# Two parts of a layer's modulation move into another stage, and their working room with them

## The chip, the core and the metric

The kernel runs on one core of a Trainium2 chip. Its engines work side by side, each through its own queue in order: TensorE (PE) does the matmuls, VectorE (DVE) and ScalarE (ACT) do element-wise work, GpSimd (POOL) takes some of it from VectorE, and SyncE (SP) issues nearly all transfers. The metric is the device time of one execution in microseconds, and lower is better.

## The reference, cut to what matters

One transformer block (gated delta net and dilated attention, then a feed-forward part) is followed by two layers on a stream of 512 tokens and a context of 256 tokens, both 1024 wide. Each of the two layers is modulated by six vectors, which come from a condition vector c for the stream and another for the context:

```python
for layer in range(DEPTH_2):
    mod_l = (jax.nn.silu(c) @ w_ada[layer] + b_ada[layer])[:, None, :]
    mod_c = jax.nn.silu(c_ctx) @ w_ada[layer] + b_ada[layer]
    sh1_l, sc1_l, g1_l, sh2_l, sc2_l, g2_l = jnp.split(mod_l, 6, axis=-1)
    ...
    h_l = modulate(x_l, sh1_l, sc1_l)     # rms_norm(x) * (1 + scale) + shift
    h_c = modulate(x_c, sh1_c, sc1_c)
    ...                                   # mixer: layer 0 even, layer 1 odd
    x_l = x_l + g1_l * y_l
    x_l = x_l + g2_l * conv_ffn(modulate(x_l, sh2_l, sc2_l), ...)
```

The product with w_ada is a matrix (6144 x 1024) times two vectors. All values are float32.

## The kernel before

**Layout and matmuls.** Streams lie feature-major: 1024 features are eight tiles of 128 partitions, with tokens along the free side. A float32 product is made of three matmuls of split values (high by high, high by low, low by high), lines L323, L324 and L325 in `mm3`. `wchunk` fetches 128x1024 weights (512 KB) into `wraw` (two buffers) and splits them into `whi` (ACT, L311) and `wlo` (POOL, L312; three buffers each). A chunk serves 24 matmuls of 512 columns.

**Stages in order.** `block1_mixer` makes the first block's projections and its two attentions. Behind the delta net's projections stand `dilated_bias` (a table that goes through DRAM into `dstrip`, 2 MB), `hyena_mlp` (three rounds of a small matmul, a sine whose argument is reduced by seven DVE steps, and ACT's sine `fh`; its weights are `fw`) and `dilated_proj` (`dq`, `dk` by DVE, `dv` by ACT). `block1_tail` makes the context's normalised and modulated input `hc`, the hyena filter's taps (`hyena_taps`), the output projection (`out_proj`), the norm behind it (`post_norm`, with two spectra of the taps on PE), and the first feed-forward part: four groups of 6, 6, 5 and 5 hidden tiles, each with its gate and up products (24 matmuls each) and then eight down products. In this part `x` is the residual stream, 16 KB a partition, that the part's own norm adds to at its end. `even_mixer` follows: six projections token-major (`qk_gemm` and `qk_post` for queries and keys, with squares on ACT L1361 and their sums on DVE L1363), then the attentions. Then come `out_and_ffn` for layer 0, the odd mixer, and `out_and_ffn` for layer 1.

**The modulation.** `ada(pool, parts)` is a generator. It loads c for both streams to all partitions (1 MB), makes the silu (four steps on ACT L1081 and DVE L1082), and for each part (a third of a layer: 16 tiles of 128 outputs) fetches 32 pieces of w_ada of 256 KB and reduces each with both vectors on DVE (L1090: `ada_j` and `ada_w` are the two outputs, which nobody reads; the sum goes to `ada_p`). A part has 64 reductions in 16 steps of four. Three buffers of `ada_w` turn round, so a load on SP waits for a reduction.

**Beside.** `with self.beside(steps, rate, skip)` makes each `wchunk` that ticks add `rate` to a count, and each whole unit takes a step of the generator. `issue_after` keeps the step's instructions behind the latest instruction of their engine at that point. What is left at the end of the `with` is emitted there. The tile framework orders instructions by a simulated timeline, so the order on an engine isn't only that of the program. Before, part (0,0) runs beside `dilated_proj` at 4 steps a tick, parts (0,1) and (0,2) beside the even mixer's projections at 3 a tick, and layer 1's three parts beside layer 0's `out_and_ffn` at 0.8 a tick.

Of the kernel before, what the change touches and what calls it, by code (L numbers as in the profile page):

```python
# [2 lines left out]

# [219 lines left out]
class Prog:  # L223
# [225 lines left out]
    def block1_mixer(self, hp, psd):  # L449
        V, S, G, PE, Q, A = self.V, self.S, self.G, self.PE, self.Q, self.A  # L450
        h = hp.tile([P, 2, KD, T], F32R, name="h", tag="hx")
        with self.pools(p1=1) as (pp,):
            rb = pp.tile([P, T], F32, name="rb")
            with self.pools(g0=1) as (gp,):
                es = ExitStack()
                self.banks = {"mm": 4, "g": 4, "p": 3, "c": 1, "o": 1, "a": 2, "pv": 1}
                with self.pools(psA=1) as (ps,):
                    act = self.acts(h, 0, T)
                    da = self.pool(es, "da")
                    with self.pools(ad=1, gp1=1) as (ad, gt), ExitStack() as xs:  # L460
                        xp = self.pool(xs, "x0", side="right")
                        x = xp.tile([P, KD, T], F32, name="x")
                        acc = xp.tile([P, T], F32, name="acc")
                        Q.dma_start(self.sm, A["small"])
                        first = [self.wchunk(A["w1_qkv"][0], eng=V)]
                        for k in range(KD):
                            (Q if k % 2 else S).dma_start(x[:, k], A["xT"][k * P:(k + 1) * P])
                        first.append(self.wchunk(A["w1_qkv"][1]))
                        for k in range(KD):
                            g = self.vec("g_mix_pre", k)  # L470
                            S.activation(h[:, 0, k], x[:, k], AF.Copy, scale=g)
                            V.scalar_tensor_tensor(out=h[:, 1, k], in0=x[:, k], scalar=g,
                                                   in1=h.bitcast(F32)[:, 0, k], op0=ALU.mult, op1=ALU.subtract)

                        def stats():
                            self.load_consts()
                            for k in range(KD):
                                accs = self.sqacc(xp, acc, x[:, k], k, eng=V, bufs=2)
                            r = self.token_rstd(pp, ps, accs, 4, "g")
                            pb = self.bank(ps, "g")  # L480
                            self.bcast_all(pb, r, 4)
                            S.activation(rb, pb, AF.Copy)
                            return r

                        r = self.gdn(gp, gt, ps, rb, stats, act, self.tiles_of(h), first)
                        self.dilated_bias(ps)
                        with self.beside(self.ada(ad, [(0, 0)]), 4, 0, self.mark):
                            self.tick()
                            with self.pools(hm=1) as (hm,):
                                self.hyena_mlp(hm, ps)  # L490
                            self.dilated_proj(da, ps, rb, r, act, self.tiles_of(h))
                om = hp.tile([P, 2, KD, T], F32R, name="h", tag="hx")
                with self.pools(psA2=1, gt=1) as (ps, gt):
                    with self.pools(db2=1) as (db,), ExitStack() as pd:
# [25 lines left out]
    def gdn(self, gp, gt, ps, rb, stats, act, tiles, first):  # L520
# [49 lines left out]
        for mi in range(12):  # L570
# [2 lines left out]
            conv(mi)  # L573
            if mi == 1:
                self.gdn_gates(gp, gt, ps, rb, act)
            if mi == 11:
                self.mark = self.latest(V)
            if mi:
                turn(mi - 1)
        sg = self.sg = gp.tile([P, 4, T], F32, name="sgate")  # L580
# [391 lines left out]
    def block1_tail(self, hp, ps, om, begun, x, hc):  # L972

        V, S, G, PE, Q, A = self.V, self.S, self.G, self.PE, self.Q, self.A
        with self.pools(t1=1, tt=2) as (tp, tt):
            es = ExitStack()
            hf = self.pool(es, "hf")
            y = tp.tile([P, KD, T], F32, name="y")
            xc = y[:, 0:4].rearrange("p a (b t) -> p (a b) t", b=2)
            Q.dma_start(xc, A["cT"].rearrange("(k p) t -> p k t", p=P))  # L980
            accc = hf.tile([P, C], F32, name="accc")
            for k in range(KD):
                accs = self.sqacc(tt, accc, xc[:, k], k)
            self.modulate(tt, ps, xc, accs, hc, 0, 0, 1)
            self.hyena_taps(tp, hf, ps)
            acc = tp.tile([P, T], F32, name="acc")
            act = self.acts(om, 0, T)
# [23 lines left out]
            es.close()  # L1011
            tf = self.pool(es, "tf", 2)
            act = self.acts(h, 0, T)
            m0 = 0
            for ng in FFN_GROUPS:
                fa = []
                for m in range(m0, m0 + ng):
# [14 lines left out]
                    self.split(a[:, 0], a[:, 1], g)  # L1032
                    fa.append((a[:, 0], a[:, 1]))
                last = m0 + ng == MF
                for m in range(KD):
                    w = self.wchunk(A["w1_d"][m][:, m0 * P:(m0 + ng) * P], ng * P)
                    p = self.bank(ps, "mm")
# [10 lines left out]
            self.dump("x1", x)  # L1048
            es.close()
            return r  # L1050

    def post_norm(self, tt, ps, accs, acc, y, x, rp, spec, then=None):

# [14 lines left out]
        return r  # L1068


    def ada(self, pool, parts):

        V, S, Q, A = self.V, self.S, self.Q, self.A
        c = pool.tile([P, 2, D], F32, name="ada_c")
        junk = pool.tile([P, T], F32, name="ada_j")
        raw = lambda: pool.tile([P, T], F32, name="ada_w", bufs=3)
        Q.dma_start(c.rearrange("p s k -> p (s k)"), A["c_row"].to_broadcast([P, 2 * D]))
        for s in range(2):
            for i in range(2):
# [46 lines left out]
    def modulate(self, tt, ps, x, accs, h, layer, i0, s, r=None, st="t"):  # L1126
# [1 line left out]

        V, S = self.V, self.S
        mod = self.mods[layer]  # L1130
        n = x.shape[2]
        if r is None:
            r = self.token_rstd(tt, ps, accs, n // P, st)
        rb = self.bank(ps, st)
# [1 line left out]
        for k in range(KD):  # L1136
            tmp = tt.tile([P, T], F32, name="md")
            sh = mod[:, i0 * 8 + k, s:s + 1]
            V.scalar_tensor_tensor(out=tmp[:, :n], in0=x[:, k], scalar=mod[:, (i0 + 1) * 8 + k, s:s + 1],
                                   in1=rb[:, :n], op0=ALU.mult, op1=ALU.mult)  # L1140
            S.activation(h[:, 0, k], tmp[:, :n], AF.Identity, bias=sh)
            V.scalar_tensor_tensor(out=h[:, 1, k], in0=tmp[:, :n], scalar=sh, in1=h.bitcast(F32)[:, 0, k],  # L1142
# [279 lines left out]
    def even_mixer(self, hp, ps, psd, hs, first):  # L1422
# [5 lines left out]
        with self.pools(em=1) as (em,):  # L1428
# [12 lines left out]
            with self.pools(ei=1, et=2) as (ei, tt):  # L1441
# [12 lines left out]
                for g, dst, gain, tab in ((0, qa, gq, None), (1, ka, gk, None), (3, qkb, dq, tq), (4, qkb, dk, tk),  # L1454
# [25 lines left out]

                        post = None
                    jobs.append((gemm, post))
                with self.pools(ad2=1) as (ad,), self.beside(self.ada(ad, [(0, 1), (0, 2)]), 3):
                    self.pipeline(jobs)
            psd.close()
            oms = [self.new_h(hp, s) for s in range(2)]
# [593 lines left out]
```

## Time and profile before

| | us |
|---|---|
| median of 3 runs | 2619.76 (2618.95 to 2622.86) |
| the profiled execution | 2619.97 |
| its span in the profile | 2618.2 |
| PE busy | 2474.6 (95%) |
| DVE busy | 1631.3 (62%) |
| ACT busy | 993.6 (38%) |
| POOL busy | 1194.1 (46%) |
| reductions of the modulation on DVE | 189.7 + 179.9 |

The span is what the trace covers. The busy shares are means over stages that differ, so stages are read one by one. A wait names the engine or transfer that came last.

### The profile page before, as it was taken

To read this page: it belongs to the slowest core of one execution; us is meant where nothing else is said; L and a number is where in the kernel's file an instruction comes from. 1 tells how busy PE (TensorE), PEld (TensorE's weight loads), DVE (VectorE), ACT (ScalarE), POOL (GpSimd) and SP (SyncE) were. 2 spreads that over 40 slices of the span, in tenths; PEclk is the share of its full clock that TensorE was granted. 3 is DMA by queue.
4 is the path that set the end of the run, shared out by engine and by line. 5 is a ranking of instruction groups with operands and counts; after the bars stand their busy time and mean duration, and the time that the engine had idled before them with its cause. 6 is when DMAs were issued, how large, how long until landed. Compare 5 with 4: busy or idle time off the path is not lost.

```text
span 2618.2 us, 35313 instructions
## 1 busy us (share of the span) xinstructions
PE 2474.6 (95%) x13312; PEld 2051.2 (78%) x13312; DVE 1631.3 (62%) x2896; ACT 993.6 (38%) x1763; POOL 1194.1 (46%) x835
## 2 busy tenths in 40 slices
PE   7888999899999988987999999999999999999999
PEld 5766876788888766766788888888888888788887
DVE  6987656645334698868747677868667456534333
ACT  4434534422224422367734212122234563323232
POOL 3346535555556444577724233333245427344443
PEclk9988999899999998998999999999999999999999
DMA  5252022222322333400132333434232114232322
GB/s 197 73 187 67 26 63 97 81 93 92 104 94 91 141 129 126 164 15 26 51 113 97 107 132 117 132 108 140 87 115 84 49 42 142 84 97 87 103 94 96
DMA packets 103453, 257.94 MB, mean 99 GB/s; under 512 B 11745, under 2 KB 20065, under 8 KB 102900
## 3 DMA queue, kind: packets, MB, share of 16 engines
q1 hardware_dynamic: 102708, 254.64, 29.0%
q8 instruction: 105, 1.72, 0.3%
q10 hardware_dynamic: 576, 1.05, 0.1%
q14 instruction: 64, 0.52, 0.1%
HBM read 246.06 MB, written 14.83 MB: 100 GB/s over the span
## 4 chain that ended last, share of the span: by engine, by line
PE 72%; DVE 16%; DMA 3%; ACT 3%; issue 3%; POOL 3%; SPq 0%; POOLq 0%; DVEq 0%; ACTq 0%
PE ps_mm L323 14%; PE ps_mm L325 14%; PE ps_mm L324 14%; PE ps_mx L324 3%; PE ps_mx L325 3%; PE ps_mx L323 3%; PE ps_m L324 3%; PE ps_m L323 3%; PE ps_m L325 3%; PE ps_pv L1596 2%; DVE ada_j L1090 2%; PE ps_s L1589 2%; DVE ada_w L1090 2%; PE ps_t L435 2%; DMA ada_w<-in_w_ada 2%
## 5 line engine op out<-in xcount | busy, mean ns | idle before, releaser
L312 POOL TENSOR_TENSOR wlo<-wraw,whi 128x1024 fp32r<-128x1024 f32 (+2 forms) x344 | 778.0, 2265 | 1102.7 <-ACT whi L311 1026.8
L311 ACT ACTIVATE whi<-wraw 128x1024 fp32r<-128x1024 f32 (+2 forms) x345 | 336.9, 978 | 949.0 <-PE ps_mm L324 480.9
L323 PE MATMUL ps_mm<-h,whi 128*128 128x512 f32 (+1 forms) x1496 | 541.3, 363 | 11.8 <-ACT whi L311 7.2
L325 PE MATMUL ps_mm<-h,wlo 128*128 128x512 f32 (+1 forms) x1496 | 540.4, 362 | 2.0 <-POOL wlo L312 2.0
L324 PE MATMUL ps_mm<-h,whi 128*128 128x512 f32 (+1 forms) x1496 | 540.5, 362 | 1.1 <-DVE h L1142 1.0
L323 PEld LDWEIGHTS ps_mm<-h,whi 128*128 128x128 f32 x1496 | 282.8, 189 | 56.9 <-ACT whi L311 7.2
L325 PEld LDWEIGHTS ps_mm<-h,wlo 128*128 128x128 f32 x1496 | 282.4, 189 | 48.9 <-POOL wlo L312 2.6
L324 PEld LDWEIGHTS ps_mm<-h,whi 128*128 128x128 f32 x1496 | 282.5, 189 | 47.6 <-issue 1.7
L1090 DVE CUSTOM_DVE_ANT_0 ada_j<-ada_w,ada_c 128x512 f32<-128x512 f32 x192 | 189.7, 988 | 13.7 <-DMA ada_w<-in_w_ada 13.3
L324 PE MATMUL ps_mm<-fa,whi 128*128 128x512 f32 (+1 forms) x528 | 187.6, 356 | 0.0
L325 PE MATMUL ps_mm<-fa,wlo 128*128 128x512 f32 (+1 forms) x528 | 186.3, 356 | 1.0 <-POOL wlo L312 1.0
L323 PE MATMUL ps_mm<-fa,whi 128*128 128x512 f32 (+1 forms) x528 | 185.8, 356 | 0.0
L1090 DVE CUSTOM_DVE_ANT_0 ada_w<-ada_w,ada_c 128x512 f32<-128x512 f32 x192 | 179.9, 937 | 4.0
L1267 DVE SCALAR_TENSOR_TENSOR cb<-ps_mm,small,cb 128x511 f32<-128x511 f32 (+1 forms) x66 | 43.6, 661 | 191.2 <-ACT cb L1265 191.1
L1215 DVE SCALAR_TENSOR_TENSOR x<-ps_mm,mod,x 128x512 f32<-128x512 f32 x80 | 59.5, 748 | 137.1 <-PE ps_mm L325 130.2
L325 PEld LDWEIGHTS ps_mm<-fa,wlo 128*128 128x128 f32 x528 | 99.0, 188 | 17.6 <-POOL wlo L312 1.6
L323 PEld LDWEIGHTS ps_mm<-fa,whi 128*128 128x128 f32 x528 | 98.9, 188 | 16.4 <-ACT whi L311 0.3
L324 PEld LDWEIGHTS ps_mm<-fa,whi 128*128 128x128 f32 x528 | 99.2, 188 | 16.0
L435 PE MATMUL ps_t<-ident,E 128*128 128x128 f32 x464 | 78.8, 289 | 19.2 <-POOL E L1771 13.4
L903 DVE TENSOR_REDUCE nm<-ps_s 128x1 f32<-128x768 f32 (+1 forms) x96 | 74.1, 774 | 28.4 <-PE ps_s L1589 27.1
L324 PE MATMUL ps_mx<-h,whi 128*128 128x512 f32 x216 | 86.3, 399 | 3.2 <-DVE h L1002 3.2
L323 PE MATMUL ps_mx<-h,whi 128*128 128x512 f32 x216 | 85.6, 398 | 0.5 <-ACT whi L311 0.5
(498 smaller groups left out, 5178.5 us busy)
## 6 DMA issues: line engine op xcount, KB each, us to landing
ada_w<-in_w_ada SPq DMA_DIRECT2D x192, 256.0 KB
wraw<-in_w_up SPq DMA_DIRECT2D x88, 512.0 KB
wraw<-in_w_d SPq DMA_DIRECT2D x48, 384.0 KB
wraw<-in_w_d SPq DMA_DIRECT2D x53, 320.0 KB
wraw<-in_we_in SPq DMA_DIRECT2D x24, 512.0 KB
wraw<-in_w_g SPq DMA_DIRECT2D x22, 512.0 KB
wraw<-in_w_u SPq DMA_DIRECT2D x22, 512.0 KB
wraw<-in_we_out SPq DMA_DIRECT2D x13, 512.0 KB
```

Of the source, the lines that this page charges most:

```text
L311: self.S.activation(hi[:, :n], raw[:, :n], AF.Copy)
L312: (eng or self.G).tensor_tensor(out=lo[:, :n], in0=raw[:, :n], in1=hi.bitcast(F32)[:, :n], op=ALU.subtract)
L323: mm(ps, lhi, rhi, start=start, stop=False)
L324: mm(ps, lhi, rlo, start=False, stop=False)
L325: mm(ps, llo, rhi, start=False, stop=stop)
L435: last = self.PE.transpose(ps[:, j * P:(j + 1) * P], src[:, j * P:(j + 1) * P], self.ident)
L903: V.tensor_reduce(out=m, in_=src, op=ALU.max, axis=AX.X, negate=True)
L1090: V.tensor_tensor_reduce(out=(junk, w)[s], in0=w, in1=c[:, s, i * T:i * T + T], scale=0.5, scalar=0.0, op0=ALU.mult, op1=ALU.add, accum_ou ...
L1215: V.scalar_tensor_tensor(out=xs[s][:, m], in0=p[:, :w], scalar=mod[:, gate * 8 + m, s:s + 1], in1=xs[s][:, m], op0=ALU.mult, op1=ALU.add)
L1267: V.scalar_tensor_tensor(out=cb[:, t0 + 1:t1], in0=pg[s][:, :w_ - 1], scalar=fw[0], in1=cb[:, t0 + 1:t1], op0=ALU.mult, op1=ALU.add)
L1589: self.PE.matmul(p[:, c0:min(n, c0 + 512)], q[i], k[i][:, c], start=i == 0, stop=i == 1)
L1596: self.PE.matmul(pv[64 * e:64 * e + 64, cols], vals(e, kt), pts[e][:, kt * P:(kt + 1) * P], start=kt == 0, stop=kt == nk - 1)
```

## The change

Part (0,0) leaves `block1_mixer`, and part (0,1) leaves `even_mixer`. Both now run beside the first feed-forward part, at 0.52 steps a tick after two ticks. There `x` is written to DRAM (`x_away`) ahead of the part, `ada` uses x's tiles as its room (four for c, one for `ada_j`, three for `ada_w`), and ahead of the last group's down products `x` is read back. The context's normalisation and modulation, which need part (0,0), move from the start of `block1_tail` to that same place, with the context in two tiles of the `fa` tag. Part (0,2) stays beside the even mixer's projections at 1.1 steps a tick.

```diff
@@ block1_mixer
-                    with self.pools(ad=1, gp1=1) as (ad, gt), ExitStack() as xs:
+                    with self.pools(gp1=1) as (gt,), ExitStack() as xs:
...
                         self.dilated_bias(ps)
-                        with self.beside(self.ada(ad, [(0, 0)]), 4, 0, self.mark):
-                            self.tick()
-                            with self.pools(hm=1) as (hm,):
-                                self.hyena_mlp(hm, ps)
-                            self.dilated_proj(da, ps, rb, r, act, self.tiles_of(h))
+                        with self.pools(hm=1) as (hm,):
+                            self.hyena_mlp(hm, ps)
+                        self.dilated_proj(da, ps, rb, r, act, self.tiles_of(h))
@@ gdn
-            if mi == 11:
-                self.mark = self.latest(V)
@@ block1_tail
             y = tp.tile([P, KD, T], F32, name="y")
-            xc = y[:, 0:4].rearrange("p a (b t) -> p (a b) t", b=2)
-            Q.dma_start(xc, A["cT"].rearrange("(k p) t -> p k t", p=P))
-            accc = hf.tile([P, C], F32, name="accc")
-            for k in range(KD):
-                accs = self.sqacc(tt, accc, xc[:, k], k)
-            self.modulate(tt, ps, xc, accs, hc, 0, 0, 1)
             self.hyena_taps(tp, hf, ps)
...
             act = self.acts(h, 0, T)
+
+            away = self.dp.tile([D, T], F32, name="x_away")
+            for k in range(KD):
+                Q.dma_start(away[k * P:(k + 1) * P], x[:, k])
+            side = ExitStack()
+            side.enter_context(self.beside(self.ada(tp, [(0, 0), (0, 1)], x), 0.52, 2))
             m0 = 0
             for ng in FFN_GROUPS:
...
                 last = m0 + ng == MF
+                if last:
+                    side.close()
+                    for k in range(KD):
+                        Q.dma_start(x[:, k], away[k * P:(k + 1) * P])
+                    self.context_in(tt, tf, ps, hc)
                 for m in range(KD):
...
+    def context_in(self, tt, tf, ps, hc):
+
+        xs = [tf.tile([P, 4, C], F32, name="xc", tag="fa", bufs=7) for _ in range(2)]
+        for i, xc in enumerate(xs):
+            self.Q.dma_start(xc, self.A["cT"][i * T:(i + 1) * T].rearrange("(k p) t -> p k t", p=P))
+        acc = tf.tile([P, C], F32, name="accc", tag="fth")
+        for k in range(KD):
+            accs = self.sqacc(tt, acc, xs[k // 4][:, k % 4], k)
+        self.modulate(tt, ps, xs, accs, hc, 0, 0, 1)
@@ ada
-    def ada(self, pool, parts):
+    def ada(self, pool, parts, room=None):
...
+        else:
+            c = room[:, 0:4].rearrange("p (s a) t -> p s (a t)", s=2)
+            junk = room[:, 4]
+            slots = itertools.cycle(room[:, i] for i in (5, 6, 7))
+            raw = lambda: next(slots)
@@ even_mixer
-                with self.pools(ad2=1) as (ad,), self.beside(self.ada(ad, [(0, 1), (0, 2)]), 3):
+                with self.pools(ad2=1) as (ad,), self.beside(self.ada(ad, [(0, 2)]), 1.1):
                     self.pipeline(jobs)
```

`modulate` also takes the context as a list of two tiles now.

## Rows read from the trace of the kernel before

**Rows 1.** The page's part 4: the chain that ended last, by engine.

```profile
PE 72%; DVE 16%; DMA 3%; ACT 3%; issue 3%; POOL 3%; SPq 0%; POOLq 0%; DVEq 0%; ACTq 0%
```

**Rows 2.** Windows: stretch, length, busy (count) of PE, PEld, DVE, ACT, POOL; clock; DMA; GB/s.

```profile
130.00:230.00 100.00, 79.55 (x304) 59.56 (x304) 91.67 (x185) 27.70 (x40) 44.15 (x27) 0.87 0.46 160
424.00:470.00 46.00, 42.10 (x155) 28.28 (x153) 43.45 (x62) 26.66 (x47) 25.78 (x13) 0.93 0.23 79
500.00:850.00 350.00, 350.00 (x1535) 286.05 (x1534) 143.25 (x128) 103.38 (x133) 188.31 (x101) 1.00 0.29 95
905.00:1130.00 225.00, 195.53 (x855) 158.42 (x853) 189.82 (x352) 75.32 (x132) 111.80 (x55) 0.93 0.36 126
1460.00:1890.00 430.00, 430.00 (x2493) 378.37 (x2492) 311.35 (x578) 104.18 (x127) 134.60 (x59) 1.00 0.37 122
```

**Rows 3.** Lines, 905 to 1130, DVE: count, busy, mean ns, idle before.

```profile
L1090 DVE CUSTOM_DVE_ANT_0 ada_w<-ada_w,ada_c 128x512 f32<-128x512 f32 x64 | 58.4, 912 | 1.4
L1090 DVE DVE_READ_ACCUMULATOR2_ANT ada_p<- 128x1 f32 x128 | 10.3, 81 | 0.0
```

**Rows 4.** Waits, 125 to 235, PE: total, times, longest.

```profile
PE ps_g L1890 <- DMA fw<-in_hy_w: 9.4, 1, 9.4
PE ps_p L435 <- ACT dv L890: 4.8, 1, 4.8
PE ps_mm L323 <- DVE dk L888: 3.2, 1, 3.2
PE ps_g L1890 <- ACT fh L1900: 2.2, 1, 2.2
```

**Rows 5.** Waits of SP's own queue, 100 to 235.

```profile
SPq L1088 <- DVE ada_p L1090: 56.8, 28, 4.8
```

**Rows 6.** Timeline of PE: start, length, line, shapes.

```profile
149.13 0.39 PE L324 MATMUL ps_mm<-h,whi 128*128 128x512 f32 x1
149.36 0.39 PE L325 MATMUL ps_mm<-h,wlo 128*128 128x512 f32 x1
...
162.84 0.79 PE L325 MATMUL ps_mm<-h,wlo 128*128 128x512 f32 x1
...
166.84 0.63 PE L325 MATMUL ps_mm<-h,wlo 128*128 128x512 f32 x1
```

**Rows 7.** Lines, 424 to 440, DVE.

```profile
L1142 DVE SCALAR_TENSOR_TENSOR h<-md,mod,h 128x256 fp32r<-128x256 f32 x8 | 6.8, 885 | 0.2 <-ACT h L1141 0.2
L1139 DVE SCALAR_TENSOR_TENSOR md<-y,mod,ps_t 128x256 f32<-128x256 f32 x8 | 3.6, 475 | 4.6 <-PE ps_t L431 4.6
```

**Rows 8.** Timelines of PE and of DVE.

```profile
455.41 0.40 PE L325 MATMUL ps_m<-h,wlo 128*128 128x512 f32 x1
...
471.32 4.87 DVE L1061 TENSOR_TENSOR y<-y,ps_t 128x512 f32<-128x512 f32 x8 [1.31 <-PE ps_t L431]
```

**Rows 9.** Waits, 870 to 1100, PE.

```profile
PE ps_mx L323 <- ACT qk_raw L1362: 20.3, 3, 9.0
PE ps_t L1411 <- DVE qk_raw L1398: 5.0, 2, 2.7
```

**Rows 10.** Lines, 1460 to 1890, DVE.

```profile
L1090 DVE CUSTOM_DVE_ANT_0 ada_j<-ada_w,ada_c 128x512 f32<-128x512 f32 x96 | 103.0, 1073 | 1.0 <-DMA ada_w<-in_w_ada 0.9
```

**Rows 11.** Lines, 500 to 850, DVE.

```profile
L1028 DVE SCALAR_TENSOR_TENSOR fg<-fth,fg 128x512 f32<-128x512 f32 x22 | 46.9, 2134 | 16.9 <-ACT fth L1027 16.9
L1025 DVE TENSOR_TENSOR fg<-ps_mx,rb 128x512 f32<-128x512 f32 x22 | 15.1, 689 | 40.0 <-PE ps_mx L325 40.0
```

**Rows 12.** Waits of SP's own queue, 1460 to 1890.

```profile
SPq L1088 <- DVE ada_p L1090: 229.1, 91, 8.5
```

**Rows 13.** Windows: the start, and the first feed-forward part's end.

```profile
5.00:10.00 5.00, 2.62 (x5) 1.19 (x6) 3.54 (x5) 4.57 (x9) 0.00 (x0) 1.00 1.05 397
820.00:852.00 32.00, 32.00 (x140) 25.79 (x139) 8.05 (x11) 15.79 (x23) 22.01 (x15) 1.00 0.33 101
```

**Rows 14.** Timeline of POOL.

```profile
407.67 4.83 POOL L517 TENSOR_TENSOR accc<-accc,sq 128x256 f32<-128x256 f32 x6 [7.25 <-ACT sq L514]
```

More of the change, by code (lines that the diff above doesn't have):

```diff
@@ L1 @@
+import itertools
 import math
@@ L1068, in post_norm @@
         return r
-    def ada(self, pool, parts):
+    def ada(self, pool, parts, room=None):
         V, S, Q, A = self.V, self.S, self.Q, self.A
-        c = pool.tile([P, 2, D], F32, name="ada_c")
-        junk = pool.tile([P, T], F32, name="ada_j")
-        raw = lambda: pool.tile([P, T], F32, name="ada_w", bufs=3)
+        if room is None:
+            c = pool.tile([P, 2, D], F32, name="ada_c")
+            junk = pool.tile([P, T], F32, name="ada_j")
+            raw = lambda: pool.tile([P, T], F32, name="ada_w", bufs=3)
+        else:
[3 more added lines that the diff above has]
+            raw = lambda: next(slots)
         Q.dma_start(c.rearrange("p s k -> p (s k)"), A["c_row"].to_broadcast([P, 2 * D]))
@@ L1130, in modulate @@
         mod = self.mods[layer]
-        n = x.shape[2]
+        parts = x if isinstance(x, list) else [x]
+        n, each = parts[0].shape[2], KD // len(parts)
         if r is None:
@@ L1138, in modulate @@
             sh = mod[:, i0 * 8 + k, s:s + 1]
-            V.scalar_tensor_tensor(out=tmp[:, :n], in0=x[:, k], scalar=mod[:, (i0 + 1) * 8 + k, s:s + 1],
+            V.scalar_tensor_tensor(out=tmp[:, :n], in0=parts[k // each][:, k % each],
+                                   scalar=mod[:, (i0 + 1) * 8 + k, s:s + 1],
                                    in1=rb[:, :n], op0=ALU.mult, op1=ALU.mult)
```

## The prediction

> **What bounds the kernel now.** I read the chain of waits first: TensorE's own work holds 72% of it and VectorE's 16% [rows 1], so some 420 us of the 2618.2 us hang on VectorE, and the question is where. The table of windows answers that [rows 2]. In F (500 to 850, the first feed-forward part) PE is busy 350.00 of 350 us at clock 1.00, and DVE only 143.25. In A (130 to 230, the first mixer's last projections) DVE is busy 91.67 of 100, and PE only 79.55 at a mean clock of 0.87. E (905 to 1130, the even mixer's projections) looks alike: DVE 189.82 of 225, PE 195.53, clock 0.93. C (424 to 470) has DVE at 43.45 of 46. G (1460 to 1890, the second feed-forward part, with three parts of the modulation beside it) is the comparison for F: DVE 311.35 of 430, and PE still 430.00 of 430 at 1.00. So VectorE paces A, C and E, and TensorE alone paces F and G; the modulation's reductions stand in A and E where VectorE is full. Last I read PE's waits in A and E, to see what a full VectorE costs there.
>
> **A loses part (0,0).** It goes out with 64 reductions, 32 loads of 256 KB, the 1 MB load of c and its four products. At 912 ns for one and 0.08 us for its readout, as E's rows have them [rows 3], that is some 63 us of DVE's 91.67. PE's waits that lead back to it [rows 4]: 9.4 us for the MLP's weights fw, small loads that stand on SP behind loads of ada_w, and SP waited 56.8 us in all for reductions to free their buffers [rows 5]; 4.8 us for dv, whose copy on ACT stands behind fh, which waits for the sine's steps on DVE; 3.2 us for dk, a DVE step; 2.2 us for fh. Sum 19.6. After a stall the matmuls start 0.43 us apart instead of 0.23, TensorE's 1.2 GHz level instead of 2.4 [rows 6]: 10 in the stretch shown, and two more stretches of 8; 26 x 0.20 = 5.2 us, and I add 2 for the transposes after the last stall. Recoverable: 27. I leave 2 for the last copy of dv, which the next pool's banks wait for in any case, and 3 because the 2 MB copy that makes dstrip still stands ahead of fw. A: -22. Bounds: -27, and -10 if the fw wait stays whole with its slow matmuls and 5 us of the rest.
>
> **C loses the context's modulation.** 16 DVE steps, 6.8 + 3.6 = 10.4 us [rows 7]. PE ended the output projection at 455.8, and the post norm's first DVE step over y came at 471.32 [rows 8]; in between DVE worked off what had queued. With 10.4 us less in a full DVE that step comes up to 10 earlier. PE has 48 spectrum matmuls of its own there (11 us), which cover some of the wait now. C: -7; bounds -2 and -10. The few matmuls for the context's statistics only move, and count nothing.
>
> **E loses part (0,1), and (0,2) goes from 3 steps a tick to 1.1.** 64 reductions at 0.99 us [rows 3] are 63 us of DVE's 190, and what a tick puts into DVE's queue falls from 12 reductions (12 us) to 4 or at times 8. PE waited 20.3 us, three times, for a bank that ACT had not emptied [rows 9]: ACT's squares wait for DVE to reduce the square before, and that reduction stands behind the burst. Another 5.0 us went to qk_raw itself. The three waits left 13, 11 and 8 matmuls at 0.43 us: 32 x 0.20 = 6.4. Recoverable: 31.7. A tick's 4 reductions still stand in the same queue, and so do c's four products, so I take three quarters: -24. Bounds: -10, if stalls shrink by no more than DVE's work does (63 of 190: a third), and -32.
>
> **F gains parts (0,0) and (0,1).** 128 reductions, 64 loads of 256 KB, one of c; 0.52 steps for each weight chunk, so after some 64 of the 68 chunks ahead of the last down products all 32 steps are out. The cover is DVE's 207 idle us. By G's 1073 ns [rows 10] plus the 0.08, 128 x 1.15 = 147 us, and DVE stands at 290 of 350. But F is not G: POOL is busy 188.31 of 350 us (54%) in F and 134.60 of 430 (31%) in G [rows 2], and DVE steps with two operands in SBUF wait for POOL's. L1028 (fth and fg from SBUF) takes 2134 ns where L1025 of the same size (one operand a bank) takes 689 [rows 11]. The reductions have both operands in SBUF. G's surplus of 0.38 us, raised by 54/31, makes 1.36 + 0.08 us each, 184 us in all, and DVE at 327 of 350. That still fits. Queued behind a reduction are the steps that make fa, on which the next down products wait, and banks, of which there are six, three pairs. SP: a load of ada_w waits for its buffer and holds the weights behind it. In G these waits were 229.1 us in sum [rows 12], and PE lost nothing, as weights are fetched five chunks ahead (two raw, three split). F: +2 for the four group ends; bounds 0 and +66 (the first rival).
>
> The Trainium skill (SBUF — State Buffer, section "Who interferes with whom") says that a VectorE instruction with two SBUF inputs and a GpSimd instruction that reads SBUF shut each other out for a whole instruction. This trace agrees, by the 2134 against 689 ns. By that rule F would hold POOL's 188, 30 for the 44 fa and L1028 steps and 88 for the reductions at their bare length, 306 of 350, and the sum would stay as it is.
>
> **F's end takes over the context, and x comes back.** Writing x away (2 MB) falls in F's first 25 us, where only the weights move. At the end 2 MB of x and 1 MB of context go ahead of the last weights on SP: 8 us at the 397 GB/s that the start of the kernel shows [rows 13], 19 at A's 160. The weights are up to five chunks of 3.4 to 5.5 us ahead, so most is covered. POOL takes six adds of the context (4.83 us [rows 14]) on top of 22.01 in 32, DVE the 10.4 on top of 8.05 [rows 13]; both fit, POOL closely, and the last normalisation waits for POOL's adds. +3; bounds 0 and +10. At the start of the kernel the 1 MB load of c leaves a full DMA; I find no PE wait that ends with it, so 0, bound -3.
>
> **Sum.** -22 - 7 - 24 + 2 + 3 = -48, against the profiled execution's own 2619.97 us (span 2618.2, 1.8 around it); the median of the runs is 2619.76, the same. 2572.
>
> **Rivals.**
> 1. VectorE becomes F's bound, and the kernel is slower. If each reduction waits for POOL as L1028 does, 128 x 2.13 = 273 us on 143 make 416 in 350: F grows by 66, and the time is 2572 - 2 + 66 = 2636. The change breaks even where a reduction costs (350 + 50 - 143)/128 = 2.0 us. For it: the same kind of operands, and a POOL that is more in use than in G. Against it: in G the mean was 1073 because after one wait several reductions run one behind the other, where L1028 waits alone each time. Chance 0.07; with milder lengthening it ends near the old time.
> 2. SP's queue in F does what it did in A: loads of ada_w, held by late reductions, hold back weights. A paid 9.4 + 2 once for 16 steps; F has 32, so twice that: 2572 + 23 = 2595. For it: the reductions will be slower than in G. Against it: G's 229.1 us of such waits cost PE nothing. Chance 0.16.
> 3. The stalls in A and E are not the bursts but the chains themselves (the sine's three rounds, POOL's rope products), and A and E give their low bounds: 2572 + 12 + 14 = 2598. For it: POOL shares E's chain. Against it: DVE is 92% and 84% busy there. Chance 0.12.
> 4. All goes by the high bounds: -27 - 10 - 32 - 3 = -72, 2548. Chance 0.10.
>
> **How the numbers follow.** The forecast holds 0.55, from 2556 to 2586 by A and E's bounds taken halfway. Below 2550 lies half of rival 4 (0.05), above 2604 rival 1 (0.07) and the tails of 2 and 3, where they come together (0.06); the range is 2550 to 2604. A measurement of this kernel can tell some 0.2%, 5 us, from no change. Slower takes most of rival 1, 0.05; the same 0.03, from rival 1's milder end and the tails of 2 and 3; faster 0.92.
>
> **What would show it.** Right: A without PE's waits for fw and dv and about 22 us shorter; E with PE's waits for qk_raw L1362 under 6 us and DVE under 65%; the post norm's first step over y some 7 us nearer to the end of the output projection; F with PE still busy throughout at 1.00, DVE above 80%, the reductions at 1.1 to 1.5 us. Wrong: reductions in F near 2 us, PE waiting there for fa, or for whi with a load behind it; PE waiting for w_d as x comes back; or E's waits for qk_raw unchanged at half the reductions.

## The result

The changed kernel takes 2578.01 us (median of 4 runs, 2577.48 to 2578.90) against 2619.36 us before (4 runs, 2617.32 to 2622.86): a ratio of 0.9841, 95% interval 0.9824 to 0.9858, so 41 us faster. The forecast was 2572 in 2550 to 2604. The profiled execution has a span of 2576.3 us, 41.9 less than before.

First the page's chain that ended last, by engine, of the changed kernel; it answers to [rows 1]: VectorE's share fell from 16% to 14%.

```profile
PE 74%; DVE 14%; POOL 3%; issue 3%; ACT 3%; DMA 2%; SPq 0%; POOLq 0%; DVEq 0%; ACTq 0%
```

Where the 41.9 us come from is read from marks: one instruction that begins each stage in both traces. The table gives the time between marks. The first mark is the first step that writes `cv_y`, then the first transposition of `gdn` (the end of A), the last row of products into `ps_o` (the end of the recurrences), the first post norm's pass over y (after C), the second post norm's pass over y (after F), and the first product into `ps_s`.

| stage | before | after | change | forecast |
|---|---|---|---|---|
| start to cv_y | 39.4 | 37.6 | -1.8 | 0 |
| cv_y to gdn's transpositions (A) | 190.8 | 170.2 | -20.5 | -22 |
| recurrences, to the last ps_o | 167.0 | 162.2 | -4.9 | 0 |
| to the first pass over y (C) | 74.1 | 65.4 | -8.7 | -7 |
| to the second pass over y (F) | 389.7 | 407.9 | +18.2 | +5 |
| to the first ps_s (E) | 264.5 | 243.2 | -21.3 | -24 |
| the rest | 1492.7 | 1489.9 | -2.8 | 0 |

Windows of the changed kernel, with the columns of [rows 2]: A, C, F from the first group to the fourth, and E.

```profile
127.00:208.00 81.00, 75.89 (x312) 57.82 (x313) 31.84 (x51) 25.30 (x36) 41.09 (x28) 0.96 0.27 93
371.00:435.00 64.00, 63.24 (x258) 46.05 (x257) 44.44 (x61) 28.25 (x45) 34.47 (x17) 0.97 0.33 111
485.00:795.00 310.00, 305.03 (x1323) 249.37 (x1321) 235.36 (x373) 83.90 (x104) 168.12 (x84) 0.99 0.48 153
843.00:1086.00 243.00, 226.49 (x1009) 184.11 (x1009) 169.79 (x266) 88.05 (x151) 124.03 (x66) 0.96 0.33 109
```

In A, VectorE went from 91.67 busy us of 100 to 31.84 of 81, and in E from 84% to 70%. In F it is at 76%, and PE, which was full before, lost 5 us in this window alone.

Waits of the changed kernel (engine, what it waited for, total, times, longest), from A, F, F's end, E, and SP's queue in F:

```profile
PE ps_g L1911 <- DMA fw<-in_hy_w: 4.5, 1, 4.5
...
PE ps_p L436 <- ACT dv L887: 0.6, 1, 0.6
...
PE ps_mx L324 <- ACT fa L319: 4.3, 1, 4.3
...
PE ps_t L413 <- DVE ms L415: 4.2, 1, 4.2
PE ps_t L432 <- DVE rsq_i L302: 0.9, 1, 0.9
...
PE ps_mx L324 <- ACT qk_raw L1383: 0.8, 1, 0.8
...
SPq L1107 <- DVE ada_p L1109: 100.8, 60, 4.5
```

Against [rows 4], fw fell from 9.4 to 4.5 and dv from 4.8 to 0.6, and the waits for dk and fh are gone. Against [rows 9], the wait for a bank of qk_raw fell from 20.3 to 0.8; the one for qk_raw itself only fell from 5.0 to 3.9, and the waits for its transposed copies (kaT and qaT) rose from 2.3 to 5.2. New are the wait for fa, in F's first group, and the wait behind `ms`, in the normalisation at F's end. Loads of ada_w waited 100.8 us on SP for reductions, and PE waited for no transfer in F.

In F the sequence of PE's products gives the lengths of the parts, first product to last:

| part of F | before | after |
|---|---|---|
| gate and up, group 1 | 77.3 | 78.1 |
| down, group 1 | 33.4 | 41.1 |
| groups 2 and 3, gate and up | 65.1, 54.2 | 65.1, 54.2 |
| groups 2 and 3, down | 33.4, 27.8 | 33.4, 27.8 |
| gate and up, group 4 | 54.2 | 54.2 |
| down, group 4 | 27.8 | 30.3 |
| spectrum beside the last normalisation, 48 products | 14.5 | 21.7 |

So F's 18 us stand in two places, 8.6 us at the first group and 9.6 us at the end, and nothing is lost in between. Only 20 of the 128 reductions run before the first group's stall; the other 108 cost PE nothing.

VectorE's lines in F, after (count, busy, mean ns), beside [rows 10] and [rows 11], and the window ahead of the first group's end:

```profile
L1109 DVE CUSTOM_DVE_ANT_0 x<-x 128x512 f32<-128x512 f32 x128 | 126.7, 1010 | 1.9
...
L1025 DVE SCALAR_TENSOR_TENSOR fg<-fth,fg 128x512 f32<-128x512 f32 x22 | 30.6, 1392 | 15.9 <-ACT fth L1024 15.9
...
497.00:529.00 32.00, 28.48 (x124) 22.81 (x122) 29.79 (x52) 7.79 (x11) 15.94 (x9) 0.99 0.49 156
```

A reduction took 1010 ns, where the forecast had 1.36 us. The timeline of the two places (start, length):

```profile
530.45 0.80 PE L324 MATMUL ps_mx<-fa,whi 128*128 128x512 f32 x1 [4.25 <-ACT fa L319]
531.05 0.63 PE L326 MATMUL ps_m<-fa,wlo 128*128 128x512 f32 x1
531.48 0.63 PE L324 MATMUL ps_m<-fa,whi 128*128 128x512 f32 x1
...
816.77 2.68 POOL L516 TENSOR_TENSOR acc<-acc,sq 128x512 f32<-128x512 f32 x2
...
816.86 1.22 DVE L301 TENSOR_TENSOR rsq_a<-rsq_i,rsq_a 128x2 f32<-128x2 f32 x1
...
819.50 2.31 DVE L301 TENSOR_TENSOR rsq_a<-rsq_i,rsq_a 128x2 f32<-128x2 f32 x1
...
822.11 0.16 DVE L301 TENSOR_TENSOR rsq_a<-rsq_i,rsq_a 128x2 f32<-128x2 f32 x1
...
830.54 0.68 DVE L1044 TENSOR_TENSOR y<-ps_m,y 128x512 f32<-128x512 f32 x1
...
834.46 0.15 DVE L415 TENSOR_SCALAR ms<-ps_t 128x4 f32<-128x4 f32 x1
834.76 1.83 PE L413 MATMUL ps_t<-ones,sq 128*128 128x1 f32 x8 [4.23 <-DVE ms L415]
...
843.26 4.87 DVE L1073 TENSOR_TENSOR y<-y,ps_t 128x512 f32<-128x512 f32 x8 [2.77 <-PE ps_t L432]
```

At 530 PE has waited 4.25 us for fa, and for some 5 us its matmuls then start 0.43 us apart, at the 1.2 GHz level. At the end no reduction runs any more (the last one starts at 774.5). The context's rsqrt takes until 822 (steps over two columns last 1.22 and 2.31 us beside POOL's work, 0.16 otherwise). Its modulation holds VectorE until 838, and the last add into y (830.54) and the normalisation's step `ms` (834.46) stand in the middle of it. Ahead of its second batch of statistics PE waits 4.23 us for `ms`, which reads the first batch, and then runs 12 products of the spectrum 0.43 us apart. That is most of the spectrum's 7.2 us; PE's wait for the context's own rsqrt was 0.9 us.

### The profile page after: what moved, and what is told of

Same layout as the page of the kernel before. It is cut to its first block, busy times and chain, and to the rows that moved or that the text cites. A ratio compares the mean times of both kernels' runs of the same rounds, so it can differ in the third digit from the quotient of the medians.

```text
span 2576.3 us, 35335 instructions
## 1 busy us (share of the span) xinstructions
PE 2456.0 (95%) x13312; PEld 2036.3 (79%) x13312; DVE 1637.1 (64%) x2896; ACT 995.2 (39%) x1763; POOL 1195.4 (46%) x835
## 4 chain that ended last, share of the span: by engine, by line
PE 74%; DVE 14%; POOL 3%; issue 3%; ACT 3%; DMA 2%; SPq 0%; POOLq 0%; DVEq 0%; ACTq 0%
PE ps_mm L324 15%; PE ps_mm L326 15%; PE ps_mm L325 15%; PE ps_mx L324 3%; PE ps_mx L325 3%; PE ps_mx L326 3%; PE ps_m L326 3%; PE ps_m L324 3%; PE ps_m L325 3%; PE ps_pv L1617 3%; PE ps_t L436 2%; PE ps_s L1610 2%; DVE h L1163 1%; DVE cv_y L538 1%; DVE acc L516 1%
## 5 line engine op out<-in xcount | busy, mean ns | idle before, releaser
L1109 DVE CUSTOM_DVE_ANT_0 ada_j<-ada_w,ada_c 128x512 f32<-128x512 f32 x128 | 132.7, 1036 | 5.8 <-DMA ada_w<-in_w_ada 5.5
L1109 DVE CUSTOM_DVE_ANT_0 ada_w<-ada_w,ada_c 128x512 f32<-128x512 f32 x128 | 127.9, 999 | 3.5
L1109 DVE CUSTOM_DVE_ANT_0 x<-x 128x512 f32<-128x512 f32 x128 | 126.7, 1010 | 1.9
L326 PEld LDWEIGHTS ps_mm<-fa,wlo 128*128 128x128 f32 x528 | 99.0, 188 | 17.7 <-POOL wlo L313 1.7
L900 DVE TENSOR_REDUCE nm<-ps_s 128x1 f32<-128x768 f32 (+1 forms) x96 | 73.9, 774 | 31.7 <-PE ps_s L1610 30.2
L325 PE MATMUL ps_mx<-h,whi 128*128 128x512 f32 x216 | 85.5, 396 | 3.7 <-DVE h L993 3.7
```

The lines of the kernel that those rows point to most:

```text
L325: mm(ps, lhi, rlo, start=False, stop=False)
L326: mm(ps, llo, rhi, start=False, stop=stop)
L900: V.tensor_reduce(out=m, in_=src, op=ALU.max, axis=AX.X, negate=True)
L1109: V.tensor_tensor_reduce(out=(junk, w)[s], in0=w, in1=c[:, s, i * T:i * T + T], scale=0.5, scalar=0.0, op0=ALU.mult, op1=ALU.add, accum_ou ...
```

## The experiments

Diffs are against the changed kernel. A run's time is a median, with a ratio to the kernel before; "F" is from the first gate product to the second pass over y: 384.4 us before, 402.6 in the changed kernel.

In F's length, two traces of the changed kernel differ by 0.1 us, and two other runs with the same code in F (`burst_3` and `without_02`, 400.6 and 401.1) lie up to 2 us lower.

**The context in the third group.** First theory: F's end loses its 9.6 us to the context's chain on VectorE. Rival: x's read-back.

```diff
+                if m0 == 12:
+                    self.context_in(tt, tf, ps, hc)
                 if last:
...
-                    self.context_in(tt, tf, ps, hc)
```

> Against the changed kernel only the place of the context's normalisation and modulation differs: ahead of the third group's down products, not the last group's; x is still read back ahead of the last group's. First theory: the 2.5 us that the last down products and the 7.1 us that the last normalisation take longer than before are the context's chain on VectorE (its rsqrt steps and 16 modulation steps stand in front of the adds into y). Then those 9.6 us come back, less 0 to 2 us in the third and fourth group: 2569 (2567 to 2572). Rival: x's read-back, 2 MB ahead of the last weights on SP and ahead of the last addition, is what costs: 2577 to 2579, and the last normalisation as long as in the changed kernel.

Measured: 2581.25 us, ratio 0.9857 (0.9824 to 0.9891); F 400.1. The end was mended as the theory had it (last down products 27.8, spectrum 14.5), with x's read-back where it was. But 7.3 us were lost elsewhere: the third group's down products took 29.1 instead of 27.8, the fourth group's gate and up products 60.2 instead of 54.2. Its windows over the third group's down products and then the fourth group:

```profile
712.00:750.00 38.00, 38.00 (x171) 30.99 (x171) 19.55 (x37) 14.58 (x26) 21.32 (x15) 1.00 0.40 133
750.00:795.00 45.00, 41.24 (x174) 33.23 (x173) 44.05 (x80) 11.23 (x15) 21.61 (x10) 0.96 0.49 166
```

`issue_after` keeps a step behind the latest VectorE instruction, and that was now the modulation's last one. So no reduction ran from 714 to 750, and then 32 in 43 us: VectorE at 44.05 of 45, as in the first group of the changed kernel. The expected time was missed, but the cause held: the loss at the end comes from the context and not from x's read-back. With no reductions beside it the whole context cost the third group 1.3 us.

**A later start.**

```diff
-            side.enter_context(self.beside(self.ada(tp, [(0, 0), (0, 1)], x), 0.52, 2))
+            side.enter_context(self.beside(self.ada(tp, [(0, 0), (0, 1)], x), 0.6, 12))
```

> Against the changed kernel the modulation starts 12 ticks into the first feed-forward part instead of 2, at 0.6 steps a tick instead of 0.52. First theory: the 8.6 us that the first group loses (PE waits 4.3 us for fa, then runs at the lower clock) come from c's silu and some 26 reductions that crowd VectorE while it makes that group's fa; begun under the down products they stand beside one step of VectorE per output, and the later groups, which lost nothing at 0.52, lose 0 to 2 us at 0.6: 2570 (2568 to 2573). Rival: the reductions are too dense for VectorE wherever they start, so the stall moves to the second group's fa: 2577 to 2586, with PE waiting for fa there.

Measured: 2573.09 us, 0.9829 (0.9798 to 0.9859), an interval that overlaps the changed kernel's, so the reading rests on F: 394.5, 8.1 less. The first group's down products take 33.4 us again. VectorE is fuller than in the changed kernel in the middle, and from the modulation's start to the last group's down products PE doesn't wait:

```profile
505.00:535.00 30.00, 30.00 (x132) 24.40 (x131) 17.50 (x19) 7.50 (x10) 14.26 (x9) 1.00 0.31 93
545.00:785.00 240.00, 240.00 (x1051) 196.95 (x1050) 196.45 (x321) 65.21 (x79) 131.85 (x64) 1.00 0.49 165
```

So 82% of VectorE over 240 us costs nothing, and 30 us at 93% ahead of a group's end (29.79 of 32 us from 497 to 529 in the changed kernel) cost 8. The first theory holds for the first group, the rival (too dense wherever they start) falls. F's end is no better: the last down products take 32.4 us and the spectrum 21.3.

**One part alone.** In `mixer_keeps_00` part (0,0) and the context's modulation are as before and (0,1) alone runs in F. In `even_keeps_01` it is (0,0) and the context that are in F, and the even mixer has its two parts at 3 a tick.

```diff
# mixer_keeps_00, with part (0,0) beside dilated_proj and the context at the tail's start again
+            side.enter_context(self.beside(self.ada(tp, [(0, 1)], x), 0.26, 2))
...
-                    self.context_in(tt, tf, ps, hc)
# even_keeps_01
+            side.enter_context(self.beside(self.ada(tp, [(0, 0)], x), 0.26, 2))
...
+                with self.pools(ad2=1) as (ad,), self.beside(self.ada(ad, [(0, 1), (0, 2)]), 3):
```

> Part (0,0) stays in the first mixer and the context's modulation at the start of the tail, as before; part (0,1) alone goes into the first feed-forward part at 0.26 steps a tick, x goes out and comes back as in the changed kernel, and part (0,2) stays beside the even mixer at 1.1. First theory: the first mixer, the output projection's stage and the start give back 19 + 9 + 3 us (and up to 5 more in the recurrences); the end of the first feed-forward part has x's read-back but no context, and its 9.6 us come back; the first group loses 4 instead of 8.6 us, as the silu stays and the reductions are half as dense: 2578 + 31 - 9.6 - 4.6 = 2595 (2592 to 2601). Rival, x's read-back is what costs at the end: 2605 (2602 to 2611).

> Part (0,0) and the context go into the first feed-forward part as in the changed kernel, at 0.26 steps a tick; parts (0,1) and (0,2) stay beside the even mixer's projections at 3 steps a tick, as before. First theory: the even mixer gives back its 21 us, PE's waits for qk_raw return to about 20, the first group loses 4 instead of 8.6, the end of the first feed-forward part stays 9.6 longer: 2578 + 21 - 4.6 = 2594 (2590 to 2599). Rival: the even mixer's gain came with the time at which it starts and with its clock rather than from the reductions taken out of it: 2574 to 2580.

Measured: `mixer_keeps_00` 2593.77 us, 0.9912 (0.9889 to 0.9935); F 384.5, the 384.4 of before to 0.1 us, with 64 reductions and x out and back in it; A 189.9 us, as long as before.

```profile
490.00:850.00 360.00, 360.00 (x1586) 294.59 (x1585) 200.96 (x269) 108.66 (x139) 199.19 (x103) 1.00 0.37 123
```

That settles x's read-back: it costs nothing. `even_keeps_01` 2599.83 us, 0.9933 (0.9906 to 0.9960); F 393.4: no loss at the first group, and 8.6 us at the end, where the context is. E took 270.6 us instead of 243.2, and PE's wait for qk_raw is back. (That is 6 us more than before the change, with much the same waits and a mean granted clock of 0.91 for 0.93, and the run came out just above the expected range; why the clock differs is open.)

```profile
PE ps_mx L324 <- ACT qk_raw L1383: 18.7, 3, 8.7
```

I had expected half of the first group's loss in both; there was none. That both make c's silu as early as the changed kernel does clears the silu by itself; it was the density of the reductions: 8 from 497 to 529 in `even_keeps_01`, 20 in the changed kernel (the two rows in this order). F starts 5 us later in the first, so the fair count, over 32 us from each kernel's own first reduction, is 10 against 20.

```profile
L1109 DVE CUSTOM_DVE_ANT_0 x<-x 128x512 f32<-128x512 f32 x8 | 10.1, 1278 | 0.1
```

```profile
L1109 DVE CUSTOM_DVE_ANT_0 x<-x 128x512 f32<-128x512 f32 x20 | 20.0, 1023 | 0.1
```

**Burst or amount in the even mixer.**

```diff
# burst_3
-                with self.pools(ad2=1) as (ad,), self.beside(self.ada(ad, [(0, 2)]), 1.1):
+                with self.pools(ad2=1) as (ad,), self.beside(self.ada(ad, [(0, 2)]), 3):
# without_02, in ada: zeros in ada_p for part (0, 2)
-            for b in range(16):
+            for b in range(0 if room is None and parts == [(0, 2)] else 16):
```

> Against the changed kernel only the rate of part (0,2) beside the even mixer differs: 3 steps a tick instead of 1.1. If the burst (12 reductions in VectorE's queue at a tick) made the even mixer's waits, half of them come back in the first half of the projections: PE's waits for qk_raw at 8 to 12 us, 2578 + 11 = 2589 (2584 to 2595). If the number of reductions made them, 64 in either case, nothing changes: 2576 to 2581.

> Against the changed kernel part (0,2) leaves out its 64 reductions and 32 loads (zeros in their place), so that the even mixer's projections have no modulation beside them but c's silu. If reductions are still what the even mixer waits for, the rest of the 31.7 us that the prediction called recoverable comes, 31.7 - 21.3 = 10: 2568 (2565 to 2572). If the waits left there are the mixer's own chains, 2575 to 2579.

Measured: `burst_3` 2590.65 us, 0.9916 (0.9893 to 0.9938), E 258.3; `without_02` 2564.33 us, 0.9813 (0.9796 to 0.9830), E 229.9. The burst is what made the waits, and more than I expected: 17.7 us where I had 8 to 12. Without (0,2) E lost 13 us more, where I had 10. PE's wait in E for a bank of qk_raw in the one, and for qk_raw in the other:

```profile
PE ps_mx L324 <- ACT qk_raw L1383: 17.7, 2, 9.0
```

```profile
PE ps_t L1434 <- DVE qk_raw L1421: 1.4, 1, 1.4
```

The same 64 reductions cost 28 us at 3 steps a tick (258.3 - 229.9) and 13 at 1.1 (243.2 - 229.9). So of E's 21 us, 15 are the rate and only the rest the part that left.

**Every reduction twice.**

```diff
+                        if room is not None:
+                            V.tensor_tensor_reduce(out=junk, in0=w, in1=c[:, s, i * T:i * T + T], scale=0.5,
...
```

> Against the changed kernel each of the 128 reductions beside the first feed-forward part is made twice, with the same loads. If VectorE has the room that its busy share shows and no more (234 us of the 310 us from 485 to 795), 128 further reductions at 1.07 us make 371 us, the first feed-forward part grows by about 61 us, and PE waits for fa in each group: 2639 (2620 to 2650), slower than the kernel before. If loads on SP pace that part, or VectorE's busy time is waiting that two reductions can share, 2580 to 2605.

Measured: 2639.06 us, 1.0091 (1.0073 to 1.0110), slower than before; F 456.4. Window, VectorE's lines and PE's waits:

```profile
500.00:800.00 300.00, 259.70 (x1074) 205.56 (x1073) 278.22 (x530) 63.20 (x79) 141.96 (x66) 0.95 0.37 124
```

```profile
L1113 DVE CUSTOM_DVE_ANT_0 x<-x 128x512 f32<-128x512 f32 x128 | 141.3, 1104 | 2.4
L1110 DVE CUSTOM_DVE_ANT_0 x<-x 128x512 f32<-128x512 f32 x128 | 122.2, 955 | 2.0
```

```profile
PE ps_mx L326 <- POOL wlo L313: 22.2, 11, 3.8
PE ps_mx L324 <- ACT fa L319: 17.3, 3, 8.8
```

VectorE's busy share foretold the loss well: F grew by 53.8 us, where I had 61. PE's largest sum is not for fa but for the weights' low part `wlo`; POOL, which makes it, waited 63.4 us for VectorE's fg from 500 to 800, so this too may be VectorE's lateness, which is argued and not shown. With 1.09 us of reduction for each pair of inputs the kernel takes 2578, with 2.22 it takes 2639. A straight line between them, which is an estimate, reaches the 2614.3 of before in these runs at some 1.8 us, where the prediction's first rival broke even at 2.0.

**The context without the crowd.** `stats_early_late` and `paced` both have the late start. The first moves only the context's loads, squares and rsqrt to the third group. The second moves all of it and pins the reductions behind the step ahead of it (`self.mark = self.latest(V)`). `paced_fw` adds the MLP's weights ahead of the dilated bias, and `changed_again` is the changed kernel on the same chip.

```diff
# paced
+                if m0 == 12:
+                    self.mark = self.latest(V)
+                    self.context_in(tt, tf, ps, hc)
# paced_fw
-                        self.dilated_bias(ps)
                         with self.pools(hm=1) as (hm,):
                             self.hyena_mlp(hm, ps)
+                        self.dilated_bias(ps)
```

> The late start (12 ticks, 0.6 a tick) and, of the context, its loads, squares and rsqrt ahead of the third group's down products, its 16 modulation steps still ahead of the last group's. First theory: at the end the context is late because its loads, squares and rsqrt come first, and its modulation then falls behind the down products; with them out of the way the modulation runs under the last down products, these take 27.8 us again and the last normalisation's spectrum 14.5, and the third and fourth group lose 0 to 2 us: 2573 - 8 = 2565 (2562 to 2569). Rival: the 16 modulation steps themselves keep the adds into y waiting, wherever the rsqrt is: 2571 to 2575, the spectrum still near 21 us.

> Late start (12 ticks, 0.6 a tick), the whole of context_in ahead of the third group's down products, and the reductions of those eight ticks kept behind VectorE's step before context_in instead of behind the modulation's last one. First theory: the two earlier versions lost 6 us in the fourth group because reductions queued behind the context's chain and then came in one stretch; spread again, the fourth group's gate and up products take 54.2 us, the last down products 27.8, the last spectrum 14.5, and the part from its first gate product to the second post norm's pass over y 386 to 389 us (402.6 in the changed kernel, 394.5 with the late start alone): 2566 (2562 to 2570). Rival: VectorE has no room for the context's 16 steps anywhere beside reductions at 0.6 a tick: 392 to 396 us, 2572 to 2577.

> The same, and in the first mixer the hyena MLP's weights are asked for ahead of the dilated bias and its 2 MB copy. The prediction left 3 us of PE's wait for fw in the first mixer to that copy; the changed kernel's trace shows 4.5 us. If the copy ahead of them on SP is the cause, that wait goes, with some 1 us of slow matmuls behind it: 5 us less than the run without it, 2561. If something later in the first mixer waits for the table instead (dstrip comes later), 2564 to 2570.

> The changed kernel itself, on the same chip as the two above, as the base of the comparison and for a second profile: 2578 (2574 to 2582). Stages with the same waits should agree within 1 us, but for those whose granted clock differs, the recurrences above all.

Measured: `stats_early_late` 2577.13 us, 0.9860 (0.9838 to 0.9883), F 395.0; `paced` 2571.47, 0.9844 (0.9816 to 0.9871), F 394.2; `paced_fw` 2569.24, 0.9816 (0.9791 to 0.9841), F 393.8; `changed_again` 2578.67, 0.9852 (0.9835 to 0.9868), F 402.7, so F repeats to 0.1 us. The theory missed twice. In `stats_early_late` the end's spectrum was mended (14.5), but the same crowd stood in the fourth group, 37 reductions and the 16 modulation steps, and that group took 60.5 us for 54.2 and the last down products 30.9 for 27.8:

```profile
744.00:805.00 61.00, 57.77 (x247) 46.55 (x246) 56.30 (x108) 16.51 (x24) 27.07 (x13) 0.97 0.52 171
```

Spreading the reductions did mend the fourth group in `paced` (54.9 us, the end 27.8 and 14.5), and 8 us turned up in the third group's down products instead (35.8 for 27.8):

```profile
PE ps_t L432 <- DVE rsq_i L302: 3.8, 1, 3.8
```

That is the broadcast of the context's rsqrt, which stands in PE's own queue in front of products that could run; for 3 us after it the matmuls start 0.43 us apart instead of 0.23. F's 394.2 us is what the rival had forecast (392 to 396). In `paced_fw` the 4.5 us wait for fw went, a new one of 2.3 us for fh came, and A took 169.5 us against 171.1. The time is not the 2561 that I expected; it can't be told from that of `paced`, 2 us above it.

**The rsqrt where VectorE is empty.** The last version computes the context's rsqrt ahead of the first group, with the late start and the weights' order of `paced_fw`, and loads the context a second time at the end for the 16 modulation steps.

```diff
+            rc = self.context_rstd(tt, tf, ps)
             m0 = 0
...
-                    self.context_in(tt, tf, ps, hc)
+                    self.modulate(tt, ps, self.context_tiles(tf), None, hc, 0, 0, 1, rc)
```

> Late start (12 ticks, 0.6 a tick), the MLP's weights ahead of the dilated bias, and of the context the squares and the rsqrt ahead of the first group, where VectorE has no modulation yet; at the end the context's 1 MB is loaded a second time, and only the broadcast and the 16 modulation steps stand ahead of the last down products. First theory: what the context costs beside reductions (some 8 us in each of four places) is TensorE's wait, in its queue, for the statistics and for the rsqrt chain; without them the last down products take 28 to 29 us and the last spectrum 15 to 18, the part from its first gate product to the second post norm's pass over y 386 to 390 us (394.5 with the late start alone): 2565 (2560 to 2569). Rival: the 16 modulation steps in front of the adds into y are the cost: 393 to 396 us, 2569 to 2574.

Measured: 2560.81 us, 0.9794 (0.9771 to 0.9817), below the changed kernel's interval; F 387.4, the last down products 28.9, the spectrum 16.0. A took 165.0 us at a granted clock of 1.00 from 127 to 170, where `paced_fw` with the same code and the same waits there took 169.5 at 0.92; so of the gain on the late start, 7 us are F's and some 5 A's. PE's waits from the first group's end to the end of F are 1.1 us:

```profile
PE ps_m L326 <- POOL wlo L313: 0.6, 1, 0.6
PE ps_t L413 <- POOL acc L516: 0.5, 1, 0.5
```

The 16 steps and the broadcast are where they were, and F is 3 us longer than before. The modulation now runs from 790 to 802, under the first of the last down products, instead of from 824 to 838, into the normalisation. So at F's end it wasn't the modulation's work that cost, but that squares, statistics and rsqrt let it start so late. These moved together, with POOL's six adds, so the run doesn't say which of them it was. The other places lost differently: 8 us to PE's wait for the rsqrt beside reductions in `paced`, and mostly to crowded reductions in `context_early` and `stats_early_late`.

## Why the forecast was right, and which step was not

- **A, -22.** Measured -20.5. `mixer_keeps_00`, with part (0,0) back, has the waits back (9.9 us for fw, 7.6 for dv). What I left for fw was 4.5 us, not 3, and it went in `paced_fw`, where the weights are asked for ahead of the table and its 2 MB copy. A also differs by 4.5 us between two traces of the same code, mostly with the granted clock (169.5 in `paced_fw`, 165.0 in the last version).
- **C, -7.** Measured -8.7, inside the bounds; in `mixer_keeps_00` this stage is 74.2 us again. But the mechanism that I named, from the end of the output projection to the first pass over y, gave 4.8 us (15.5 to 10.7), not 7. The other 3.7 are the output projection itself, 58.0 to 54.3 us; around its start the granted clock was 0.55 before (384 to 402) and 1.00 after (357 to 375), and in `paced_fw`, with the context gone and the recurrences at the lower clock, it takes 56.6. So some 2.3 us of it go with the clock, which is luck.
- **E, -24.** Measured -21.3. `without_02` shows that 34.6 us were to be had (264.5 - 229.9), where the prediction had 31.7; what is left is (0,2)'s own reductions, and `burst_3` shows that the rate made most of the gain. VectorE stood at 70% there, not under 65%, and in F at 76%, not above 80%.
- **F's body, +2.** Measured +8.6: the mis-sized term. "That still fits" was worked out over 350 us, and the group that failed was one of 32 us, in which reductions stood twice as dense as in `even_keeps_01`. The sign the prediction named for itself, PE waiting for fa, is there; it isn't the first rival, as reductions were cheap. The price for one, 1.36 us by POOL's share, was wrong in the safe direction: 1010 ns, 997 with half as many (`mixer_keeps_00`), 1030 with twice as many (the mean of its two rows), 1157 at most, in the last version.
- **F's end, +3.** Measured +9.6, the other mis-sized term, if inside its bounds, and the step that failed is "both fit, POOL closely". I weighed the transfers, which cost nothing (`mixer_keeps_00`), and the busy sums of POOL and VectorE over 32 us, but not the order: squares, POOL's adds, PE's statistics and VectorE's rsqrt follow one another until 822, so the modulation comes in front of the last normalisation's steps, where PE waits 4.23 us and then runs slow. "The few matmuls for the context's statistics only move, and count nothing" hides the same chain: in `paced` PE waits 3.8 us in its queue for the rsqrt behind them. The context's move gave at most 8.7 us in C and took 9.6 in F.
- **What made up for it.** The four stages of the sum gave 32.3 us, where I had 48; by them alone the time would have been 2587, still inside the range. The other 9.5 us I had put at 0: the start gave 1.8 (within the bound of -3; c's 1 MB no longer loads there, but `stats_early_late` starts in 40.6 us without it too), the rest 2.8, and the recurrences 4.9. That the forecast came within 6 us is in this part luck. The recurrences' gain isn't tied to the change: the same matmuls took 167, 162 and 168 us in the kernel before, the changed one and `paced_fw`, with the granted clock (third number from the end):

```profile
230.00:397.00 167.00, 158.80 (x1336) 129.91 (x1336) 92.85 (x249) 81.22 (x188) 89.88 (x116) 0.94 0.13 38
```

```profile
208.00:370.00 162.00, 153.49 (x1336) 125.88 (x1335) 92.07 (x246) 80.81 (x187) 87.97 (x114) 0.98 0.11 33
```

```profile
206.00:374.00 168.00, 159.31 (x1336) 129.04 (x1336) 92.26 (x248) 81.32 (x188) 87.97 (x114) 0.94 0.11 32
```

- **Rivals.** The second (SP's loads hold weights) didn't come: 100.8 us of waits on SP, and PE full from group 2 to group 4. The third fell with `without_02`: without reductions E's waits for qk_raw shrink to 1.4 us.

What stays open: why one trace's recurrences run at the lower clock, and whether the change makes that rarer (the kernel before has one trace here). The 2.8 us of the rest are inside what it varies by, 1484.7 to 1493.2 us over the traces of all runs.

## What to carry to other kernels

Work that fills an idle engine has to fit between deadlines, not on average: 82% busy under steady reductions cost nothing, and 93% over the 32 us ahead of one deadline cost 8 us, so start a filler where no deadline is near, and look whether a long chain holds it up and lets it go in one piece. When a chain that crosses engines is moved into a full stage, ask when its last steps can start and what they will then stand in front of, count each crossing as a wait in the in-order queue of the engine that bounds the stage, and take out the part that depends on nothing (here a rsqrt) to a place where its engine is idle. Where whole runs of one kernel differ by up to 20 us, compare stages between marks, with the granted clock beside them: F's length repeated within 2 us, but at different granted clocks A differed by 4.5 and the recurrences by 7 us.

## What the runs showed of the hardware

A VectorE step over two columns, 0.16 us by itself, took 1.2 to 2.3 us, four times in one chain, while POOL added and split, and each of the four ended within 0.05 us of the end of a POOL instruction (816.8, 818.1, 819.5 and 821.8). The rsqrt of ten steps took 7.9 us (814.57 to 822.46, with one add into y of 0.68 us among them), where ten steps over four columns took 1.7 us in the last normalisation of the last version. The Trainium skill's rule that a VectorE instruction with two SBUF inputs contends with a GpSimd instruction that reads SBUF, under an exclusive lock (SBUF — State Buffer, section "Who interferes with whom"), agrees with it: the shortest steps pay the most in proportion. The same step of the feed-forward part (L1028 before, L1025 after) took 2134 ns before, 1392 ns after and 970 ns with every reduction made twice. An explanation that fits, though no run shows it by itself: the fuller VectorE is, the later it comes to that step, and the less of its time there is waiting for POOL, so an engine's busy time before a change can hold waiting that a filler uses up.
